# Hybrid decoder step on one core: the decode update in the second half of its stage, the first output weights ahead of their inputs, the key norms' end and the last mixer tail some places later, the weight pool at lower addresses

## Chip, core and metric

The kernel runs on one core of one Trainium2 chip. The metric is the device time of one launch in microseconds (us), lower being better. The time of the kernel before is the median of three runs.

## What is computed

One inference step of two layers over 1,040 prompt tokens (16 learned meta tokens and 1,024 own ones) and 8 decode tokens, width 1,024, everything in float32. Layer 0 mixes tokens by a causal convolution module, layer 1 by RWKV-7 time mixing; each is followed by a squared-ReLU MLP of inner width 4,096. Only layer 1's mixer is touched here. Cut to what matters:

```python
def _wkv7_step(S, inp):                      # one token, per head: S is 64 x 64
    r_t, w_t, k_t, v_t, kk_t, a_t = inp
    sa = jnp.einsum('bhvk,bhk->bhv', S, -kk_t)
    S = (S * w_t[:, :, None, :] + sa[..., None] * (kk_t * a_t)[:, :, None, :]
         + v_t[..., None] * k_t[:, :, None, :])
    return S, jnp.einsum('bhvk,bhk->bhv', S, r_t)
# in _rwkv7: r, k, v, decay, a, g are projections of the shifted input
    kk = kk / jnp.maximum(jnp.sqrt(jnp.sum(kk * kk, axis=-1, keepdims=True)), L2_EPS)   # key norms
    S_final, ys = lax.scan(_wkv7_step, S0, xs)
    yn = ((y - mu) * lax.rsqrt(var + GN_EPS)).reshape(B, T, D_MODEL) * gn_g + gn_b
    out = ((yn + bonus) * g) @ w_o
# in _trunk
    h = h + out
    h = h + _sqrelu_mlp(_rmsnorm(h, norm_mlp[i]), w_mlp_in[i], w_mlp_out[i])
```

The prompt starts from a zero state; each of the 8 decode sequences brings its own state of 16 heads of 64 x 64, and takes one step of the recurrence. That one step is called the decode update below.

## The kernel before

**Matrix products.** A large product is made of three matmuls per 128 x 128 block: high half by high half, high by low, low by high (lines 187, 188, 189). A weight block of 512 KB is loaded on SP's queue into a `raw` tile (line 146), its high half is cast by ACT (`hi`, one operation, line 157), and its low half is subtracted by POOL in four operations of 256 columns (`lo`, line 162). There are five tiles of each kind, so that the load of a block on SP waits until POOL has split the block five places earlier, and all that stands behind that load on SP waits too. TensorE's instructions are called PE, VectorE's DVE, ScalarE's ACT, GpSimd's POOL, SyncE's SP.

**Order.** In layer 1 TensorE's instructions stand in the order in which the program writes them (`in_order`). The other engines' instructions are put in order by a scheduler that works on estimated times when the kernel is built. Every engine runs its queue strictly in that order, DMA issues included.

**Layer 1, first part (about 1,128 to 1,828 us).** `mixer_in(g)` makes the projections r, k, v and the small ones for the four token groups of `G1` (272, 256, 256, 264 columns). Between the projections' matmuls, at fill points, run pieces of earlier work: `tick` advances the recurrence of the prompt, which is worked out in 17 chunks (chunk 0 the meta tokens, then 64 tokens each), `invert` the small inverses that it needs, `norm_gates` the normalisation, bonus and gate of finished tokens. `keys(g)` makes the key norms of a group: squares on ACT, their sums `pn` on TensorE, then a square root, a reciprocal and the two halves `r16h`, `r16l` that `spread` later takes for `pb`. It runs one group ahead of its use. `carry["tail"]()` ends the last pair of heads of a group: it transposes v (`vt_7`), makes the 32 x 32 products of the key vectors (`nn_7`) and the bonus sums (`pk_7`), and writes them out to memory (`d_v`, `d_n`, `d_bv`).

In a chunk of the recurrence A (two banks for each four pairs of heads) are the products of the chunk's vectors; DVE masks them into `xa` and `nr` (lines 1200, 1202); `gg`, `bT`, `po`, `W`, `U`, `S` and `Y` follow on TensorE with copies on ACT and DVE and `sw` on POOL between them.

**Layer 1, second part (about 1,842 us to the end).** `mixer_out(g, ...)` loads the gated output z of a group of `G2` (328, 352, 352 columns) from memory, splits it, multiplies it by `rwkv_w_o` (`ps_oo_0` to `ps_oo_7`, eight weight blocks) and adds it to h. Then comes the MLP: 32 blocks j, for each an inner product `ps_in`, the activation `r`, `s` (line 342 on DVE, ACT), its halves `hh`, `hl` (line 141) and eight outer products `out` that DVE adds to h (line 355). Two blocks j are called a pair here: 96 matmuls of TensorE, four weight blocks, ten operations of lines 342 and 355 and two of line 141 on DVE. The first stage takes group 0 alone (`mixer_out(0)` and an MLP for it); the second makes `mixer_out(1)`, `mixer_out(2)` and one MLP for both.

At the time of the first stage the recurrence's last chunks, the decode update and most norm gates are still to be done. `filler` deals them out over 208 fill points in three streams side by side: the recurrence `until(NCH - 1)`, `decode_step()` with a budget of 82, and `norm_gates` of the groups 1 and 2. `decode_step` transposes the decode vectors (four `pdd`), then updates the state in 16 slices: nine DVE operations of 128 x 256 each (lines 1383 to 1391: seven of two tensors, `TENSOR_TENSOR`, and two reductions), one load before and one store behind on SP. Its output is needed only by the last norm gate.

Of the kernel before, what the change touches and what calls it, by code (L numbers as in the profile page):

```python
# [16 lines left out]
P = 128  # L17
D = 1024
KT = D // P
# [16 lines left out]
N2 = 352  # L36
# [12 lines left out]
def hybrid_step(tc, x_prompt, x_sample, state_conv, state_shift, state_wkv, meta_tokens,  # L49
# [8 lines left out]
    nc = tc.nc  # L58
    ctx = ExitStack()
    with ctx:  # L60
        def pool(stack, name, bufs, **kw):
            return stack.enter_context(tc.tile_pool(name=name, bufs=bufs, reuse_waits="tile", **kw))
# [46 lines left out]
        for name, ap in vecs:  # L109
            n = ap.shape[0]  # L110
# [10 lines left out]

        cur = {}

        def open_tmp(stack, nmax, tag, bufs=3, **kw):
            cur["n"] = cur["wide"] = nmax
            cur["tmp"] = pool(stack, f"tmp{tag}", bufs, **kw)
            cur["stat"] = pool(stack, f"stat{tag}", 1, **kw)

        def stat(name, tag, bufs, w=None):
            return cur["stat"].tile([P, w or cur["n"]], F32, name=name, tag=tag, bufs=bufs)  # L130
# [622 lines left out]
        def spread(ps, r, p):  # L753

            for i, part in enumerate(r):
                nc.tensor.matmul(ps, hspread[:, p].rearrange("p q i -> p (q i)"), part, start=i == 0, stop=i == 1)
# [105 lines left out]
        def proj(w, act, n, name, fill=None):  # L862
            ps = bank(f"p{name}")
            for k in range(KT):
                nc.tensor.matmul(ps[:, :n], w[:, k, :], act[k], start=k == 0, stop=k == KT - 1)  # L865
                if fill and k in (2, 5):
                    fill()
            return ps

        def keys(g, fill):  # L870

            c0, n = G1[g]
            nm = lambda s, *a: f"{s}{g}" + "".join(f"_{x}" for x in a)
            mix = prep[g][0]
            act = [mix(2, k) for k in range(KT)]
            pn = bank(nm("pn"), "x")
            add_pn = lambda: None

            def to_pn(p, sq):
                return lambda: nc.tensor.matmul(pn[:, :n], head_sel(p), sq[:, :n], start=p == 0, stop=p == KT - 1)  # L880
            for p in range(KT):
                yield
                ps = proj(next(wrkv), act, n, nm("k", p), fill)
                k_ = pr.tile([P, N1], F32, name=nm("st", p), tag="st", bufs=2)
                nc.scalar.copy(k_[:, :n], ps[:, :n])
                nc.scalar.dma_start(d_k[:, p, c0:c0 + n], k_[:, :n])
                sq = pr.tile([P, N1], F32, name=nm("sq", p), tag="rk", bufs=2)
                nc.scalar.activation(sq[:, :n], ps[:, :n], AF.Square, scale=vec("k_k", p))
                add_pn()
                add_pn = to_pn(p, sq)  # L890
            r16 = lorap.tile([P, N1], F32, name=nm("r16"), tag="lf")
            r16p = norm[g] = [lorap.tile([P, N1], F32R, name=nm("r16" + q), tag="r16" + q, bufs=2)[:, :n] for q in "hl"]
            add_pn()
            nc.vector.tensor_scalar(r16[:, :n], pn[:, :n], L2_EPS * L2_EPS, None, op0=ALU.max)
            nc.scalar.activation(r16[:, :n], r16[:, :n], AF.Sqrt)
            nc.vector.reciprocal(r16[:, :n], r16[:, :n])
            split(*r16p, r16[:, :n], nc.vector)
        carry = {"tail": lambda: None}

        def mixer_in(g, tick):  # L900
# [80 lines left out]
            gate(wg)  # L981
            carry["tail"]()
            act_v = mixed(3)
            r16p = norm.pop(g)
            ks = iter(())

            def finish(p, rk, ab, vv):
                def trace():
# [56 lines left out]
            late, later = (lambda: lambda: None), lambda: None  # L1045
            for p, rk2 in ahead_of(fetch):
                both()
                ps = proj(next(wrkv), act, n, nm("r", p), both)
                nc.scalar.copy(rk2[:, 2, :n], ps[:, :n])
                if p == 0:  # L1050
                    decay_rate(ww)
# [17 lines left out]
                later = late()  # L1069
                nkk, kp, rp = (rk2[:, i, :] for i in range(3))  # L1070
                pb = bank(nm("pb", p))
                spread(pb[:, :n], r16p, p)
                nc.vector.scalar_tensor_tensor(nkk[:, :n], kp[:, :n], nvec("k_k", p), pb[:, :n], op0=ALU.mult, op1=ALU.mult)
                nc.vector.tensor_tensor_scan(cum[:, :n], smask[:, :n], cum[:, :n], 0.0, op0=ALU.mult, op1=ALU.add)
                em = t_("em", p, "em", 2)
# [37 lines left out]
                if g < 3:  # L1113
                    if p == 0:
                        for _ in ranked(PP, prepare(g + 1)):
                            pass
                        ks = keys(g + 1, both)
                        next(ks)
                    for _ in keys_of(p):
                        next(ks, None)  # L1120
# [49 lines left out]
        def front(c):  # L1170

            xa = xas[c % 2]
            for q in range(2):
                nc.sync.dma_start(xa[HALF[q], :, q, :], d_ab[c, HALF[q], :, 0, :])
            bk = w_([P, KT, P], "bk", c)
            nc.sync.dma_start(bk[HALF[0]], d_ab[c, HALF[0], :, 1, :])
            for i in range(2):
                nc.sync.dma_start(bk[HALF[1], :, i * HS:(i + 1) * HS], d_ab[c, HALF[1], :, 1, (1 - i) * HS:(2 - i) * HS])
            nr, no = w_([P, KT, 2, HS], "nr", c, bufs=2), w_([P, KT, 32], "no", c)
            p32 = w_([P, KT, 32], "p32", c, bufs=2)  # L1180
            nc.sync.dma_start(p32, d_p[c].rearrange("k r t -> r k t"))

            vt = w_([P, KT, HS], "vt", c)
            for q in range(2):
                nc.sync.dma_start(vt[HALF[1 - q]], d_v[c * HS:(c + 1) * HS, :].rearrange("t (k q v) -> q t k v", q=2, v=HS)[q])
            yield RW[0]
            mask = lambda x: m_ar[:, x].unsqueeze(1).broadcast_to([P, 4, HS])
            for j in range(0, KT, 4):
                ps = [bank(f"A{c}{j}{q}", "w") for q in range(2)]
                for i in range(4):  # L1190
                    for q in range(2):
                        nc.tensor.matmul(ps[q][:, i * P:(i + 1) * P], bk[HALF[q], j + i, :], xa[HALF[q], j + i, q, :],
                                         start=True, stop=True, tile_position=(64 * q, 0))
                pv = [t.rearrange("p (i x) -> p i x", x=P) for t in ps]
                js = slice(j, j + 4)
                for q in range(2):
                    nc.scalar.copy(no[Q[2 * q], js, :], pv[q][Q[2 * q], :, 32:64])
                for q in range(2):
                    r_k = HALF[1 - q]
                    nc.vector.tensor_mul(xa[r_k, js, q, :HS], pv[q][r_k, :, :HS], mask(slice(0, HS))[r_k])  # L1200
                for q in range(2):
                    nc.vector.tensor_mul(nr[:, js, q, :], pv[q][:, :, HS:], mask(slice(HS, P)))
                if j == 0:
                    yield RW[1]
            x32 = w_([P, KT, 32], "x32", c)
            nc.vector.transpose(flat(x32), flat(p32))
            chunks[c] = xa, bk, nr, no, p32, x32, vt
            yield RW[2]

# [262 lines left out]
        with in_order():  # L1472
            shift_in()
            for _ in prepare(0):
                pass
            for _ in keys(0, lambda: None):
                pass
            for g in range(4):
                mixer_in(g, lambda slow=1.0: tick(g, slow))
            carry["tail"]()  # L1480
            while invert():
                pass
            advance(CHUNK_WAIT * NCH, NEED[GN_OF[0][-1]])
            for _ in ng0:
                pass
# [1 line left out]


        with ExitStack() as l1:
            open_tmp(l1, N2, "2", 3)  # L1490
            actp = pool(l1, "actp1", 1)
            open_weights(l1, 0, {"w": 5}, "f")
            residp = pool(l1, "resid1", 1)
            hidp = pool(l1, "hidp1", 2)
            open_ep(l1, "f", ey=2)
# [4 lines left out]
            def mixer_out(g, residp, actp, fill, add):  # L1500
                lo, n = G2[g]
                h1 = hl[g] = residp.tile([P, KT, cur["wide"]], F32, name=f"h1_{g}", tag="h")
                nc.sync.dma_start(h1[:, :, :n], d_h[:, :, lo:lo + n])
                z = new_acts(actp, f"z{g}", cur["wide"])
                for p in range(KT):
                    t = tt(f"zr{g}{p}", "t1")
                    nc.sync.dma_start(t[:, :n], d_z[:, p, lo:lo + n])
                    split(z[0][p][:, :n], z[1][p][:, :n], t[:, :n], nc.vector)
                for m in range(KT):
                    ps = dense(load_col(rwkv_w_o[0], m, f"wo{g}_{m}", nc.gpsimd), z, n, f"oo{g}_{m}", fill)  # L1510
                    nc.vector.tensor_add(h1[:, m, :n], h1[:, m, :n], ps[:, :n])
                    add(m, h1[:, m, :n])
                    fill()
# [57 lines left out]
            def group(g, actp, hidp, sums):  # L1571
# [2 lines left out]
                return (g, hv, n, *mlp_in(actp, hv, n, 1, f"m1{g}", sums), hidp)  # L1574


            ng2 = norm_gates(GN_OF[2])
            fill, rest = filler(2 * KT + MLP_POINTS,
                                ([until(NCH - 1)], FA * CHUNK_WAIT * (NCH - 1 - st["done"])),
                                ([decode_step()], 82), ([norm_gates(GN_OF[1]), ng2], NGA))  # L1580
            add, sums = sums_of(0)
            with in_order():
                mixer_out(0, residp, actp, fill, add)
# [61 lines left out]
```

## Time and profile before

| | before |
|---|---|
| median of three runs | 2812.3 us (2811.88 to 2817.02) |
| the profiled execution | 2817.97 us |
| its span, first to last instruction | 2816.3 us |
| TensorE busy in the span | 2661.4 us |
| DVE busy | 1776.7 us |
| POOL busy | 1499.7 us |
| ACT busy | 1180.9 us |
| mean granted TensorE clock | 0.972 |

A busy time is the union of an engine's instructions. An operation's length on DVE or POOL includes time in which it has started and is held up, so the same operation can have several lengths. Waits are put down to what came last before the engine went on.

### The profile page before, as it was taken

How to read it: one execution, taken by the hardware profiler on the slowest of the kernel's cores; microseconds unless marked ns; L12 is line 12 of the kernel's file. 1: busy time of each engine (PE TensorE's matmuls, PEld its weight loads, DVE VectorE, ACT ScalarE, POOL GpSimd, SP SyncE). 2: the span in 40 equal slices, each digit the busy share in tenths (PEclk: the TensorE clock that was granted, in tenths of full speed). 3: DMA queues.
4: the chain of work that ended last, by engine and by line, in shares of the span. 5: the costliest groups of instructions: out<-in, count | busy, mean ns of one | idle time of the engine just before them, and what ended most of it. 6: DMA issues, size and time to landing. Idle time of an engine off the chain costs nothing.

```text
span 2816.3 us, 51957 instructions
## 1 busy us (share of the span) xinstructions
PE 2661.4 (95%) x19866; PEld 2510.5 (89%) x19866; DVE 1776.7 (63%) x3518; ACT 1180.9 (42%) x2167; POOL 1499.7 (53%) x2066
## 2 busy tenths in 40 slices
PE   8999999999999899998999999978899999999998
PEld 7998999999999899787787777768789999999998
DVE  5999999996455545233756555488985554444444
ACT  5545444544355333233444453545444452222223
POOL 6676877887788775021111112365568773333332
PEclk9999999999999999999999999979999999999999
DMA  6663544454445642667767766766675642222211
GB/s 178 175 183 90 157 136 135 128 181 135 142 134 157 183 140 83 199 201 203 192 178 199 205 161 181 205 187 177 166 211 154 180 119 86 68 70 73 69 53 42
DMA packets 615863, 416.45 MB, mean 148 GB/s; under 512 B 104936, under 2 KB 558760, under 8 KB 615614
## 3 DMA queue, kind: packets, MB, share of 16 engines
q1 hardware_dynamic: 565996, 367.36, 46.2%
q10 hardware_dynamic: 41090, 19.93, 2.7%
q0 software_dynamic: 8528, 25.83, 2.6%
q8 instruction: 157, 2.57, 0.4%
q14 instruction: 92, 0.75, 0.1%
HBM read 345.60 MB, written 68.37 MB: 147 GB/s over the span
## 4 chain that ended last, share of the span: by engine, by line
PE 72%; DVE 13%; DMA 6%; issue 3%; ACT 3%; POOL 2%; SPq 0%; ACTq 0%; DVEq 0%; POOLq 0%
PE out L187 8%; PE ps_in L189 8%; PE ps_in L187 8%; PE out L189 8%; PE ps_in L188 8%; PE out L188 8%; PE pk L865 3%; PE pr L865 3%; PE pv L865 2%; DVE cv L519 1%; POOL wo_lo L162 1%; PE ps_o L189 1%; DVE tt L1153 1%; PE ps_o L188 1%; PE ps_o L187 1%
## 5 line engine op out<-in xcount | busy, mean ns | idle before, releaser
L162 POOL TENSOR_TENSOR wo_lo<-wo_raw,wo_hi 128x256 fp32r<-128x256 f32 x736 | 564.9, 799 | 259.3 <-ACT wo_hi L157 258.6
L162 POOL TENSOR_TENSOR wi_lo<-wi_raw,wi_hi 128x256 fp32r<-128x256 f32 x640 | 490.1, 798 | 285.5 <-ACT wi_hi L157 267.8
L187 PE MATMUL out<-hh,wo_hi 128*128 128x352 f32 (+2 forms) x1536 | 503.2, 328 | 20.7 <-DVE h L355 9.3
L355 DVE TENSOR_TENSOR h<-h,out 128x352 f32<-128x352 f32 (+2 forms) x768 | 387.3, 510 | 196.8 <-PE out L189 196.4
L189 PE MATMUL out<-hl,wo_hi 128*128 128x352 f32 (+2 forms) x1536 | 494.2, 324 | 7.2 <-DVE hl L141 7.2
L187 PE MATMUL ps_in<-m_h,wi_hi 128*128 128x352 f32 (+2 forms) x1536 | 496.2, 323 | 2.6 <-DVE h L355 2.6
L188 PE MATMUL out<-hh,wo_lo 128*128 128x352 f32 (+2 forms) x1536 | 496.0, 323 | 0.0
L189 PE MATMUL ps_in<-m_l,wi_hi 128*128 128x352 f32 (+2 forms) x1536 | 494.6, 322 | 0.1
L188 PE MATMUL ps_in<-m_h,wi_lo 128*128 128x352 f32 (+2 forms) x1536 | 492.7, 321 | 0.0
L519 DVE SCALAR_TENSOR_TENSOR cv<-u,wdw,cv 128x352 f32<-128x352 f32 (+2 forms) x720 | 376.5, 571 | 0.7
L157 ACT CAST wi_hi<-wi_raw 128x1024 fp32r<-128x1024 f32 x160 | 167.9, 1050 | 398.2 <-PE out L189 198.7
L157 ACT CAST wo_hi<-wo_raw 128x1024 fp32r<-128x1024 f32 x184 | 192.6, 1049 | 316.2 <-PE out L189 154.9
L187 PEld LDWEIGHTS out<-hh,wo_hi 128*128 128x128 f32 x1536 | 293.3, 191 | 26.9 <-DVE h L355 11.7
L189 PEld LDWEIGHTS out<-hl,wo_hi 128*128 128x128 f32 x1536 | 291.2, 190 | 8.9 <-DVE hl L141 8.8
L187 PEld LDWEIGHTS ps_in<-m_h,wi_hi 128*128 128x128 f32 x1536 | 290.0, 189 | 5.2 <-issue 1.7
L188 PEld LDWEIGHTS out<-hh,wo_lo 128*128 128x128 f32 x1536 | 292.8, 191 | 0.6
L188 PEld LDWEIGHTS ps_in<-m_h,wi_lo 128*128 128x128 f32 x1536 | 289.4, 188 | 0.9
L189 PEld LDWEIGHTS ps_in<-m_l,wi_hi 128*128 128x128 f32 x1536 | 288.6, 188 | 1.2 <-DVE m_l L285 0.4
L342 DVE SCALAR_TENSOR_TENSOR r<-ps_in,rs_m 128x352 f32<-128x352 f32 (+2 forms) x192 | 98.2, 515 | 243.3 <-PE ps_in L189 238.1
L141 DVE TENSOR_TENSOR hl<-s,hh 128x352 fp32r<-128x352 f32 (+2 forms) x192 | 147.9, 772 | 104.5 <-ACT hh L140 104.3
L344 ACT ACTIVATE s<-r 128x352 f32<-128x352 f32 (+2 forms) x192 | 93.6, 490 | 128.9 <-DVE r L342 128.5
L1030 POOL DMA_DIRECT2D d_n<-n x32 | 24.4, 764 | 212.9 <-DVE n L1020 141.0
(355 smaller groups left out, 4909.3 us busy)
## 6 DMA issues: line engine op xcount, KB each, us to landing
wi_raw<-in_w_mlp_in_dram SPq DMA_DIRECT2D x160, 512.0 KB
wo_raw<-in_w_mlp_out_dram SPq DMA_DIRECT2D x160, 512.0 KB
wk_raw<-in_rwkv_w_k_dram SPq DMA_DIRECT2D x32, 512.0 KB
wr_raw<-in_rwkv_w_r_dram SPq DMA_DIRECT2D x32, 512.0 KB
wv_raw<-in_rwkv_w_v_dram SPq DMA_DIRECT2D x32, 512.0 KB
d_ab<-ab POOLq DMA_DIRECT2D x32, 512.0 KB, 4.8
pg_raw<-in_conv_w_pw_dram SPq DMA_DIRECT2D x24, 512.0 KB
pa_raw<-in_conv_w_pw_dram SPq DMA_DIRECT2D x24, 512.0 KB
```

Of the source, the lines that this page charges most:

```text
L141: eng_lo.tensor_sub(lo, src, hi.bitcast(F32))
L157: nc.scalar.copy(hi[:, :a * b], raw[:, :a * b])
L162: eng_lo.tensor_sub(lo[:, cs], raw[:, cs], hi[:, cs].bitcast(F32))
L187: nc.tensor.matmul(ps, w[0], act[0], start=first, stop=False)
L188: nc.tensor.matmul(ps, w[1], act[0], start=False, stop=False)
L189: nc.tensor.matmul(ps, w[0], act[1], start=False, stop=last)
L342: nc.vector.scalar_tensor_tensor(r[:, :n], ps[:, :n], 0.0, rs()[:, :n], op0=ALU.max, op1=ALU.mult)
L344: nc.scalar.activation(s[:, :n], r[:, :n], AF.Square)
L355: nc.vector.tensor_add(hv[:, 4 * i + m, :], hv[:, 4 * i + m, :], ps[:, :n])
L519: nc.vector.scalar_tensor_tensor(acc[m][:, :n], ug[:, m, j:j + n], wdw[:, m, j:j + 1], acc[m][:, :n], op0=ALU.mult, op1=ALU.add)
L865: nc.tensor.matmul(ps[:, :n], w[:, k, :], act[k], start=k == 0, stop=k == KT - 1)
L1153: nc.vector.tensor_mul(o, ni[:, :j, j:j + 1].broadcast_to([B, j, wd]), ni[:, j:j + 1, j + 1:top].broadcast_to([B, j, wd]))
```

## The change

Five things are moved; what is computed stays the same.

1. **Decode update.** `late_start(DL)` puts 120 empty units ahead of `decode_step()`, and the stream's budget is DL + DN = 230 instead of 82, so the decode update is dealt out over the last part of the first stage.
2. **Key norms' end.** A `yield` cuts `keys` ahead of the last sum, square root, reciprocal and halves; that end runs in `first()`, at the first fill point within the r projection of the next `mixer_in`.
3. **Transposed x.** `x32` is made ahead of the masks of a chunk rather than behind them.
4. **Last mixer tail.** Four ticks of the recurrence run before the last `carry["tail"]()`.
5. **First output weights.** The weight blocks of `mixer_out` are asked for two ahead, the first two before z is loaded; the weight pool is opened directly behind the scratch pool, at lower addresses, and the pool of statistics behind it.

```diff
+        def open_tmp(stack, nmax, tag, bufs=3, stats=True, **kw):
...
+            if stats:
+                cur["stat"] = pool(stack, f"stat{tag}", 1, **kw)
...
                 add_pn = to_pn(p, sq)
+            yield
             r16 = lorap.tile([P, N1], F32, name=nm("r16"), tag="lf")
...
-            r16p = norm.pop(g)
-            ks = iter(())
+            ks, kend = iter(()), carry["keys"]
+
+            def first():
+                both()
+                next(kend, None)
...
-                ps = proj(next(wrkv), act, n, nm("r", p), both)
+                ps = proj(next(wrkv), act, n, nm("r", p), both if p else first)
...
-                spread(pb[:, :n], r16p, p)
+                spread(pb[:, :n], norm[g], p)
...
-                        ks = keys(g + 1, both)
+                        ks = carry["keys"] = keys(g + 1, both)
...
             yield RW[0]
+            x32 = w_([P, KT, 32], "x32", c)
+            nc.vector.transpose(flat(x32), flat(p32))
...
-            x32 = w_([P, KT, 32], "x32", c)
-            nc.vector.transpose(flat(x32), flat(p32))
             chunks[c] = xa, bk, nr, no, p32, x32, vt
...
-            for _ in keys(0, lambda: None):
-                pass
+            carry["keys"] = keys(0, lambda: None)
+            for _ in range(KT + 1):
+                next(carry["keys"])
             for g in range(4):
                 mixer_in(g, lambda slow=1.0: tick(g, slow))
+            for _ in range(4):
+                tick(3, 1.0)
             carry["tail"]()
...
-            open_tmp(l1, N2, "2", 3)
+            open_tmp(l1, N2, "2", 3, False)
+            open_weights(l1, 0, {"w": 5}, "f")
             actp = pool(l1, "actp1", 1)
-            open_weights(l1, 0, {"w": 5}, "f")
+            cur["stat"] = pool(l1, "stat2", 1)
...
+                block = lambda m: load_col(rwkv_w_o[0], m, f"wo{g}_{m}", nc.gpsimd)
+                ws = [block(m) for m in range(2)]
                 z = new_acts(actp, f"z{g}", cur["wide"])
...
-                    ps = dense(load_col(rwkv_w_o[0], m, f"wo{g}_{m}", nc.gpsimd), z, n, f"oo{g}_{m}", fill)
+                    if m + 2 < KT:
+                        ws.append(block(m + 2))
+                    ps = dense(ws.pop(0), z, n, f"oo{g}_{m}", fill)
...
+            DL, DN = 120, 110
+
+            def late_start(n):
+                for _ in range(n):
+                    yield 1
...
-                                ([decode_step()], 82), ([norm_gates(GN_OF[1]), ng2], NGA))
+                                ([late_start(DL), decode_step()], DL + DN), ([norm_gates(GN_OF[1]), ng2], NGA))
```

Line numbers of the kernel after are up to eleven higher: line 141 becomes 142, 342 becomes 343, 355 becomes 356, and the decode update's 1383 to 1391 become 1388 to 1396.

DVE around block 20 of the first stage's MLP, before: `r_20`, `r_21` are the activations of blocks 20 and 21, `hl` their low halves, `out_9` the outer products of the two blocks before.

```order
2825 L342 SCALAR_TENSOR_TENSOR r_20_0_23266<-ps_in_20_0_23241,rs_m_20453 128x328
2826 L141 TENSOR_TENSOR hl_20_23240<-s_20_0_23268,hh_20_23239 128x328
2827 L342 SCALAR_TENSOR_TENSOR r_21_0_23306<-ps_in_21_0_23281,rs_m_20453 128x328
2828 L355 TENSOR_TENSOR h_0_19706<-h_0_19706,out_9_0_0_23321 128x328
2829 L355 TENSOR_TENSOR h_0_19706<-h_0_19706,out_9_0_1_23329 128x328
2830 L141 TENSOR_TENSOR hl_20_23240<-s_21_0_23308,hh_20_23239 128x328
2831 L355 TENSOR_TENSOR h_0_19706<-h_0_19706,out_9_0_2_23337 128x328
```

The same place of DVE's queue in the kernel after; `t`, `sa`, `Sdec` belong to the decode update.

```order
2694 L343 SCALAR_TENSOR_TENSOR r_20_0_23175<-ps_in_20_0_23137,rs_m_20543 128x328
2695 L1388 TENSOR_TENSOR t_23247<-Sdec_23246,dq 128x256
2696 L1389 TENSOR_REDUCE sa<-t_23247 128x4
2697 L1390 TENSOR_TENSOR Sdec_23246<-Sdec_23246,dq 128x256
2698 L1391 TENSOR_TENSOR t_23247<-sa,dq 128x256
2699 L142 TENSOR_TENSOR hl_20_23136<-s_20_0_23177,hh_20_23135 128x328
2700 L1392 TENSOR_TENSOR Sdec_23246<-Sdec_23246,t_23247 128x256
2701 L1393 TENSOR_TENSOR t_23247<-dq 128x256
2702 L343 SCALAR_TENSOR_TENSOR r_21_0_23215<-ps_in_21_0_23190,rs_m_20543 128x328
2703 L1394 TENSOR_TENSOR Sdec_23246<-Sdec_23246,t_23247 128x256
2704 L356 TENSOR_TENSOR h_0_19797<-h_0_19797,out_9_0_0_23230 128x328
```

Before, the 144 decode operations stand between `r_2` and `r_14`, among those of the recurrence and the norm gates. After, they stand between `r_18` and the end of the last pair, with no recurrence and few norm gates among them: 20 to 22 for each pair.

SP's queue at the start of the first stage, before: `zr` are the eight inputs of `mixer_out(0)`, `wo_4` its fifth weight block, `ni` the inputs of the last inverses.

```order
579 L1507 DMA zr_19724<-d_z 128x328
580 L1507 DMA zr_19728<-d_z 128x328
581 L1507 DMA zr_19732<-d_z 128x328
582 L146 DMA wo_4_raw<-in_rwkv_w_o_dram 128x8x128
583 L1507 DMA zr_19736<-d_z 128x328
584 L1507 DMA zr_19740<-d_z 128x328
585 L1507 DMA zr_19744<-d_z 128x328
586 L1507 DMA zr_19748<-d_z 128x328
587 L1507 DMA zr_19752<-d_z 128x328
588 L1147 DMA ni_19568<-d_n 128x1024
```

The same place after; `wo_5` to `wo_7` are the last blocks of `mixer_out(0)`, `wi` the first of the MLP, `ey` the inputs of norm gates.

```order
580 L1518 DMA zr_19841<-d_z 128x328
581 L147 DMA wo_4_raw<-in_rwkv_w_o_dram 128x8x128
582 L147 DMA wo_5_raw<-in_rwkv_w_o_dram 128x8x128
583 L147 DMA wo_6_raw<-in_rwkv_w_o_dram 128x8x128
584 L147 DMA wo_7_raw<-in_rwkv_w_o_dram 128x8x128
585 L147 DMA wi_0_0_raw<-in_w_mlp_in_dram 128x8x128
586 L147 DMA wi_0_1_raw<-in_w_mlp_in_dram 128x8x128
587 L1152 DMA ni_19659<-d_n 128x1024
588 L1512 DMA h_0_19797<-d_h 128x8x328
589 L1437 DMA ey_0_19961<-d_y 128x512
590 L1437 DMA ey_1_20218<-d_y 128x512
591 L1518 DMA zr_19845<-d_z 128x328
```

Five weight loads, `ni`, h and two `ey` now stand between the third and the fourth input z, where one weight load stood; each of the five waits for POOL's split of the block five places earlier.

TensorE at the same boundary, after: what stands between the last `pb_7` of the projections and the first output product.

```order
8042 L757 MATMUL pb_7_19511<-r16l_18173,hspread 128x264
8043 L1265 MATMUL W_19535<-sv,xa_12568 64x64 x16
8044 L1235 MATMUL po_19557<-p_19199,gg_19427 32x32 x16
8045 L1281 MATMUL U_19589<-w_19552,p_19430 64x64 x16
8046 L1199 MATMUL A_19610<-xa_12567,bk_19578 128x128
...
8053 L1199 MATMUL A_19611<-xa_12567,bk_19578 128x128
8054 L1006 MATMUL vt_7_19628<-ident,vv_7_19477 128x128 x2
8055 L1023 MATMUL nn_7_19635<-ab_7_19527 32x32 x16
8056 L1039 MATMUL pk_7_19654<-rk_7_19525,hsum 128x264
8057 L188 MATMUL ps_oo_0_19874<-z_h_19817,wo_0_hi 128x328
```

Before, `pb_7` is followed by `vt_7`, `nn_7`, `pk_7` and `ps_oo_0` directly, and `W`, `po`, `U`, the eight A and what belongs to them come behind the fourth input of `ps_oo_0`.

More of the change, by code (lines that the diff above doesn't have):

```diff
@@ L122, in hybrid_step @@
         cur = {}
-        def open_tmp(stack, nmax, tag, bufs=3, **kw):
+        def open_tmp(stack, nmax, tag, bufs=3, stats=True, **kw):
             cur["n"] = cur["wide"] = nmax
             cur["tmp"] = pool(stack, f"tmp{tag}", bufs, **kw)
-            cur["stat"] = pool(stack, f"stat{tag}", 1, **kw)
+            if stats:
+                cur["stat"] = pool(stack, f"stat{tag}", 1, **kw)
         def stat(name, tag, bufs, w=None):
```

## The prediction

> **What bounds the kernel now.** First the page: the shares of the engines and the slices.
>
> ```profile
> span 2816.3 us, 51957 instructions
> PE 2661.4 (95%) x19866; PEld 2510.5 (89%) x19866; DVE 1776.7 (63%) x3518; ACT 1180.9 (42%) x2167; POOL 1499.7 (53%) x2066
> PE   8999999999999899998999999978899999999998
> DVE  5999999996455545233756555488985554444444
> ```
>
> TensorE sets the time, with 155 us of its span idle. The idle time is thickest in slices 27 to 29, where DVE is fullest: the start of the first stage. So next the windows, cut at the stages (engine busy times, granted clock, DMA):
>
> ```profile
> core 0: us, PE busy (x) PEld busy (x) DVE busy (x) ACT busy (x) POOL busy (x), PEclk, DMA share, GB/s
> 1360.00:1820.00 460.00, 430.89 (x4886) 357.93 (x4886) 263.30 (x598) 213.56 (x524) 87.18 (x162) 0.97 0.71 187
> 1820.00:1905.00 85.00, 63.39 (x661) 57.58 (x662) 65.53 (x124) 41.53 (x81) 50.73 (x67) 0.82 0.72 193
> 1905.00:2110.00 205.00, 182.45 (x2043) 170.70 (x2041) 182.97 (x362) 97.91 (x184) 119.38 (x136) 0.95 0.68 185
> 2110.00:2210.00 100.00, 98.30 (x651) 97.59 (x651) 51.17 (x95) 42.21 (x63) 84.37 (x112) 1.00 0.53 158
> ```
>
> The third row holds the decode update: PE idles 22.6 of 205 us at a clock of 0.95, and DVE is 89% busy. The fourth row is the second half of the stage: PE nearly full, DVE half empty, POOL 84% busy. PE's waits in the third stretch say who is late:
>
> ```profile
> PE bT L1253 <- DVE nr L1202: 9.0, 5, 3.6
> PE Y L1292 <- DVE nr L1202: 4.0, 2, 2.8
> ```
>
> 13.0 of the 22.6 us end with DVE's mask `nr`: the recurrence is behind work queued on DVE.
>
> **Decode, first half.** What leaves that stretch, from the groups of DVE in 1860 to 2110 (the first and the last of seven two-tensor lines, and both reductions):
>
> ```profile
> L1390 DVE TENSOR_TENSOR t<-Sdec,dq 128x256 f32<-128x256 f32 x16 | 10.7, 672 | 0.2
> L1389 DVE TENSOR_TENSOR Sdec<-Sdec,t 128x256 f32<-128x256 f32 x16 | 8.1, 505 | 0.1
> L1384 DVE TENSOR_REDUCE sa<-t 128x4 f32<-128x256 f32 x16 | 6.6, 412 | 0.3
> L1391 DVE TENSOR_REDUCE yd<-t 128x4 f32<-128x256 f32 x16 | 6.5, 408 | 0.2
> ```
>
> Seven lines between 8.1 and 10.7 us and two of 6.5 make 78 us in 144 operations. DVE's load falls from 183 to 105 us in 205. From 1360 to 1820, where DVE is 57% busy and the recurrence runs too, PE idles 29 us in 460, most of it for the projections' own inputs (below); so I leave 5 us of the 22.6 in place. The lower clock costs 0.05 x 182 = 9 us; fewer gaps should return 7. Gain 17.5 + 7 = 24.5 us, between 13 (the `nr` waits alone) and 31.
>
> **Decode, second half.** Here the decode update meets POOL's splits. How the same operation fares beside a split and without one, from DVE's and POOL's timeline (start, length):
>
> ```profile
> 2046.07 3.21 POOL L162 TENSOR_TENSOR wi_lo<-wi_raw,wi_hi 128x256 fp32r<-128x256 f32 x4 [2.27 <-issue]
> 2046.11 0.97 DVE L1387 TENSOR_TENSOR Sdec<-Sdec,t 128x256 f32<-128x256 f32 x1
> 2049.24 4.15 POOL L162 TENSOR_TENSOR wo_lo<-wo_raw,wo_hi 128x256 fp32r<-128x256 f32 x4
> 2053.03 0.40 DVE L1391 TENSOR_REDUCE yd<-t 128x4 f32<-128x256 f32 x1
> 2053.95 0.41 DVE L1383 TENSOR_TENSOR t<-Sdec,dq 128x256 f32<-128x256 f32 x1
> ```
>
> A two-tensor operation costs 0.41 us alone and up to about 1 us beside a split; the reduction costs 0.40 us even inside one. A batch of four splits takes 3.2 to 4.2 us here; undisturbed it takes 2.8 (row at 210.21 below). The Trainium skill ("SBUF — State Buffer", "Who interferes with whom") says that a DVE instruction with two SBUF inputs contends with a GpSimd instruction that reads SBUF, and that a reduction does not; by that rule the second half, where splits are densest, is the worse place for these operations, and these rows agree with it.
>
> The order puts 21.5 decode operations into each pair of blocks. The nearest thing in the trace is the pair from `r_12` to `r_14`, which held 21; behind it a pair without any:
>
> ```profile
> 2066.76 0.49 DVE L342 SCALAR_TENSOR_TENSOR r<-ps_in,rs_m 128x328 f32<-128x328 f32 x1
> 2087.73 0.49 DVE L342 SCALAR_TENSOR_TENSOR r<-ps_in,rs_m 128x328 f32<-128x328 f32 x1
> ...
> 2134.32 0.50 DVE L342 SCALAR_TENSOR_TENSOR r<-ps_in,rs_m 128x328 f32<-128x328 f32 x1 [3.10 <-PE ps_in L189]
> ...
> 2148.72 0.50 DVE L342 SCALAR_TENSOR_TENSOR r<-ps_in,rs_m 128x328 f32<-128x328 f32 x1 [3.10 <-PE ps_in L189]
> ```
>
> 20.97 us against 14.40. DVE ran without a gap through the first, but it also held two operations of the recurrence and four of norm gates of 512 columns, which leave; one of them, from the groups of DVE:
>
> ```profile
> L1439 DVE TENSOR_REDUCE ems<-ey 128x8 f32<-128x512 f32 x7 | 4.8, 679 | 1.3 <-DMA ey<-d_y 1.3
> ```
>
> Six at 0.68 are 4.1 us; 16.9 us remain. So DVE becomes the bound: 2.5 us more for each of 144 / 21.5 = 6.7 pairs, +17 us. Ends: without a split beside them 21.5 operations of 0.41 take 8.8 us, and the MLP's own twelve, at 0.50 as in the row at 2134.32, 6.0: 14.8 us a pair, a loss of 3; at the full 20.97 us the loss is 44. I take 17 because that pair lies nearest.
>
> The 16 loads and 16 stores of the states move along SP's queue with it, among weight loads that run five blocks (18 us of PE) ahead; the store waits for DVE, and the weights behind it have that cover. At the stage's end the last norm gates wait for the last decode slice, and the inputs of `mixer_out(1)` for those: +3 us (0 to 8; the chunk of norm gates costs 16 operations there, eleven before).
>
> **The boundary at 1830 to 1882.** Edits 4 and 5 meet here. What TensorE, SP, ACT and POOL do there now (waits; then starts and lengths):
>
> ```profile
> PE ps_oo L187 <- ACT wo_hi L157: 4.8, 1, 4.8
> PE nn L1018 <- DVE ab L1105: 3.4, 1, 3.4
> PE vt L1001 <- ACT vt L1003: 3.0, 1, 3.0
> ```
>
> ```profile
> 1832.01 5.85 SPq L1507 DMA_DIRECT2D zr<-d_z  x5
> 1841.40 0.32 SPq L1147 DMA_DIRECT2D ni<-d_n  x1
> 1841.50 4.83 ACT L157 CAST wo_hi<-wo_raw 128x1024 fp32r<-128x1024 f32 x5
> 1842.62 14.97 POOL L162 TENSOR_TENSOR wo_lo<-wo_raw,wo_hi 128x256 fp32r<-128x256 f32 x20 [2.88 <-ACT wo_hi L157]
> ```
>
> These 11.2 us of waits go: the casts of `wo` now stand ahead of those of z, and W, po, U and eight A fill the time of the v, n and k waits. But z inputs 4 to 8 stand behind five weight loads, each held by a split of an earlier block. With the splits starting at about 1833 instead of 1842.6, the fifth ends near 1847; `ni`, h, two `ey` (issue and transfer) follow, and input 4 arrives near 1857 and is split on DVE near 1860, behind inverses. TensorE, through with three inputs at about 1842, then waits some 18 us. The recurrence work that stood at 1851 to 1880 is by then done or follows with its inputs ready, so that I find both kernels at the same place, the fourth output block, near 1882: 0 us. The ends are -8 (five splits done earlier let `ni` pass earlier) and +14 (the 18 us less the 4.8 of `ps_oo`).
>
> **Key norms, x32.** What stands for their waits in the first part, in TensorE's waits:
>
> ```profile
> PE l_w L964 <- ACT lw L954: 6.7, 1, 6.7
> PE pn L880 <- ACT sq L888: 5.6, 4, 3.4
> ```
>
> The last `pn` moves 20 to 31 places later and its square is then long done: -5.6, of which some returns because the square root's table load and `r16` move into the r projection, ahead of the scan and `pb`. Together -3 (between -8 and +3). The transposed x ahead of the masks puts 0.4 us before `nr`, inside slack once DVE has room: 0.
>
> **Sum.** -24.5 + 17 + 3 + 0 - 3 = -7.5 us on the profiled execution's own 2817.97 us, which stands 5.7 above the median. I move the median by the same amount: 2812.3 - 7.5 = 2804.8 us. 0.2%, or 5.6 us, is what a measurement of this kernel can tell from no change.
>
> **The rivals.** *Slower, by a shared port in the second half.* If POOL's batches starve two-tensor operations, a pair takes the whole 20.97 us: -24.5 + 44 + 3 - 3 = +19.5, 2832 us. It decides from 18.3 us a pair on (equal to before), and it is slower by over 0.2% from 19.1. For it speaks one row of the convolution, where a two-tensor addition lasted through POOL's splits, of which the last batch is shown:
>
> ```profile
> 202.56 10.85 DVE L230 TENSOR_TENSOR acc_mu<-acc_mu,u 128x352 f32<-128x352 f32 x1
> 210.21 2.81 POOL L162 TENSOR_TENSOR pg_lo<-pg_raw,pg_hi 128x256 fp32r<-128x256 f32 x4
> ```
>
> Against it: in 2046 to 2050 no operation waited longer than one split. The same page of the skill calls the port an exclusive lock, held for the whole instruction, with the loser fully blocked. As a mechanism of this kernel, without starving: 16 splits of 0.70 and 19 two-tensor operations (17 of the decode update, two `hl`) of 0.35 make 17.9 us a pair, a loss of 23 us and a net -1, 2811 us: no change.
>
> *Slower, by late inputs.* The boundary's +14 with the rest of the sum: +6.5, 2819 us. It decides if `S`, `Y` and A of the last ticks, which stand behind the fourth input, are again what the first blocks wait for.
>
> *Faster, decode hidden.* If the splits hardly hold the operations up, a pair takes the 14.8 us above (loss 3, not 17): -21.5, 2791 us. For it: DVE is half idle there, and reductions do not suffer. Against it: the 20.97 us pair.
>
> **How the numbers follow.** Forecast 0.41, starving port 0.16, plain lock 0.14, late inputs 0.12, decode hidden 0.17. The forecast's own range is 2797 to 2810; 0.33 of its 0.41 lie below 2806.7. Faster: 0.33 + 0.17 + 0.02 of the lock = 0.52. Same: 0.08 + 0.11 + 0.02 = 0.21. Slower: 0.16 + 0.10 + 0.01 = 0.27. The range leaves out the outer part of the starving port and of the hidden decode: 2785 to 2827.
>
> **What would show it.** Right: in 1905 to 2100 waits for `nr` nearly gone and DVE near 55%; then pairs of 16 to 18 us with DVE full, POOL's batches at 3.2 us and more. Wrong: pairs of 14.4 us (decode hidden) or of 19 and more (port); first output blocks that end after 1905; a new wait of over 8 us at `mixer_out(1)`.

## The result

| | before | after |
|---|---|---|
| median of ten runs | 2815.77 us (2811.88 to 2818.16) | 2808.04 us (2803.01 to 2814.99) |
| ratio to before | 1 | 0.9973, 95% interval 0.9962 to 0.9983 |
| span of the profiled execution | 2816.3 us | 2802.6 us |

The kernel after is faster by 0.27%, or 7.7 us of the medians; the forecast was 7.5. The time forecast, 2804.8 us, lies 3.2 us under the measured median, within its range: the three runs it started from have a median of 2812.3 us, 3.5 under that of all ten. The two profiled executions lie 13.7 us apart. 3.7 to 4.2 of these arise in layer 0, where TensorE's order is the same in both, so I count them as chance.

The page of the kernel after:

```profile
span 2802.6 us, 51913 instructions
PE 2647.2 (94%) x19866; PEld 2497.0 (89%) x19866; DVE 1777.7 (63%) x3518; ACT 1183.1 (42%) x2169; POOL 1496.2 (53%) x2066
PE   8999999999999899998998999969999799999998
DVE  5999999996455545233756555576769754434444
```

A slice is 70 us long here. DVE's fullest slices were 27 to 30; now it is 31, and 27 to 30 are at 6 and 7. PE's dent of slices 27 to 29 is now slice 27 alone, the boundary, and a new one stands in slice 32, at the end of the stage. The windows of before, cut the same way in the kernel after:

```profile
1820.00:1905.00 85.00, 58.84 (x669) 53.89 (x670) 70.04 (x132) 35.54 (x68) 47.49 (x64) 0.82 0.62 170
1905.00:2110.00 205.00, 197.80 (x2083) 187.75 (x2082) 138.78 (x258) 108.26 (x199) 135.14 (x168) 1.00 0.70 190
2110.00:2210.00 100.00, 85.49 (x522) 81.08 (x521) 95.19 (x193) 34.49 (x49) 75.22 (x88) 0.94 0.57 167
```

The stretch that held the decode update has 7.2 us of idle PE instead of 22.6, at a clock of 1.00 instead of 0.95; the next has 14.5 instead of 1.7. TensorE's waits, first in 1905 to 2110, then in 2090 to 2240:

```profile
PE out L188 <- DVE r L343: 3.1, 2, 2.1
PE bT L1258 <- DVE nr L1209: 2.1, 2, 1.5
```

```profile
PE out L188 <- DVE r L343: 9.1, 7, 2.1
PE yn L1422 <- DVE ey L1451: 8.1, 1, 8.1
```

`nr` ended 13.0 us of waits and ends 2.1. In its place DVE's activation `r` is late once a pair, and the stage's last transposes wait 8.1 us for the norm gate behind the last decode slice.

Lengths of stages, from the starts of `pb` on TensorE and of `r` on DVE in each profile (us); `late_only` is the kernel before with the first edit alone, `early` the kernel after without it:

| | before | after | late_only | early |
|---|---|---|---|---|
| first to last `pb`, the projections | 639.1 | 632.7 | 639.7 | 632.7 |
| last `pb` to `r_0`, the boundary | 86.2 | 98.1 | 85.9 | 101.2 |
| `r_0` to `r_18` | 206.7 | 168.3 | 175.9 | 194.1 |
| `r_18` to `r_31` | 95.7 | 117.5 | 119.7 | 95.2 |
| `r_31` to the end | 599.2 | 601.5 | 602.8 | 599.5 |

Of the boundary's 11.9 us about 8 are work that moved: at `r_0` the kernel after has done one more round of U, S, Y and 16 A.

### The profile page after: what moved, and what is told of

Its sections match the earlier page's. It is cut to its first block, busy times and chain, and to the rows that moved or that the text cites. A ratio compares the mean times of both kernels' runs of the same rounds, so it can differ in the third digit from the quotient of the medians.

```text
span 2802.6 us, 51913 instructions
## 1 busy us (share of the span) xinstructions
PE 2647.2 (94%) x19866; PEld 2497.0 (89%) x19866; DVE 1777.7 (63%) x3518; ACT 1183.1 (42%) x2169; POOL 1496.2 (53%) x2066
## 4 chain that ended last, share of the span: by engine, by line
PE 72%; DVE 15%; DMA 6%; ACT 3%; issue 2%; POOL 1%; SPq 0%; ACTq 0%; DVEq 0%; POOLq 0%
PE ps_in L188 8%; PE out L188 8%; PE ps_in L190 8%; PE ps_in L189 8%; PE out L189 8%; PE out L190 8%; PE pk L866 4%; PE pr L866 3%; PE pv L866 2%; DVE cv L520 2%; DVE h L356 1%; PE ps_o L190 1%; DVE tt L1158 1%; PE ps_o L189 1%; PE ps_o L188 1%
## 5 line engine op out<-in xcount | busy, mean ns | idle before, releaser
L1035 POOL DMA_DIRECT2D d_n<-n x32 | 24.5, 765 | 204.6 <-DVE n L1025 130.9
```

## The experiments

Ratios are to the kernel before, with 95% intervals.

**The late start alone, and everything but it.** `late_only` is the kernel before with this, `early` the kernel after with the opposite:

```diff
-                                ([decode_step()], 82), ([norm_gates(GN_OF[1]), ng2], NGA))
+                                ([late_start(DL), decode_step()], DL + DN), ([norm_gates(GN_OF[1]), ng2], NGA))
```

> The kernel before with the decode update's late start alone. Theory: mixers and boundary as before, the first half 26 to 34 us shorter, the pairs from r_18 on at 17 to 18 us: 4 to 8 us faster than before. Rival, that late decode needs the ticks done earlier to pay: first half shorter by less than 20 us, no gain in all, or slower by up to 5 us.

> The kernel after with the decode update's late start taken out again (budget 82), the other four edits kept. Theory: late decode frees about 26 us between the first output block and r_18, and gives back 21.7 us in the pairs from r_18 to r_31; so with the decode early again the first half (r_0 to r_16) goes from 154 us back to about 180 and the pairs behind r_18 from 17.4 back to 14.4 us: 4 to 8 us slower than the kernel after, so within 3 us of the kernel before. Rival, that the gain is the mixers' (11 us earlier at the end of the projections) and late decode is worth nothing in the end: the same time as the kernel after, about 8 us faster than before.

Measured: `late_only` 2815.92 us, 0.9998 (0.9988 to 1.0007); `early` 2809.06 us, 0.9971 (0.9961 to 0.9981). The rivals' times, not the theory's: the late start alone gains nothing that can be measured, and without it the kernel keeps its gain. The reason that the rival of `late_only` gave is not what happened: both halves of the mechanism are there, with no ticks done earlier. That of `early`, a gain in the projections, is what the next experiment finds. `r_0` to `r_18` and `r_18` to `r_31`, first of before, then of `late_only`:

```profile
1914.70:2121.40 206.70, 182.55 (x2022) 171.31 (x2023) 184.06 (x369) 99.17 (x187) 124.49 (x140) 0.95 0.68 185
2121.40:2217.10 95.70, 95.70 (x640) 95.70 (x640) 44.13 (x83) 38.43 (x53) 79.49 (x108) 1.00 0.50 149
```

```profile
1914.60:2090.50 175.90, 172.35 (x2018) 163.59 (x2019) 114.59 (x221) 97.62 (x187) 112.30 (x139) 1.00 0.72 189
2090.50:2210.20 119.70, 104.40 (x655) 99.39 (x653) 111.62 (x224) 41.27 (x54) 93.69 (x113) 0.99 0.55 161
```

30.8 us are gained, 24.0 given back at once, 3.6 behind the stage. The 3.2 us that are left in this one profile are too few for the runs to tell from nothing.

**The key norms' end alone** (before with the second edit):

```diff
+            yield
             r16 = lorap.tile([P, N1], F32, name=nm("r16"), tag="lf")
...
-                ps = proj(next(wrkv), act, n, nm("r", p), both)
+                ps = proj(next(wrkv), act, n, nm("r", p), both if p else first)
```

> The kernel before with the second edit alone: the key norms' last sum, square root, reciprocal and halves at the first fill point of the next group's r projection. Theory, that this edit carries most of the gain: the four waits for pn (5.6 us) go and nothing comes back for them, the projections take 633 us from the first to the last pb instead of 639, and the kernel is 5 to 8 us faster than before, about as fast as the kernel after. Rival, that the square root's table load and r16 only come late elsewhere: 0 to 3 us faster.

Measured: 2808.32 us, 0.9964 (0.9951 to 0.9978). This edit alone gains as much as the whole change does. The third group's projections, of before and then of `keys_only`:

```profile
1527.30:1730.70 203.40, 185.46 (x2023) 154.36 (x2022) 113.65 (x254) 94.57 (x224) 31.48 (x51) 0.95 0.69 180
```

```profile
1526.10:1725.60 199.50, 184.18 (x2023) 153.41 (x2022) 115.45 (x258) 94.73 (x225) 31.21 (x51) 0.96 0.69 184
```

Every group is shorter, by 1.6, 2.1, 3.9 and 1.1 us. The row `pn <- ACT sq` (5.6 us) is gone from TensorE's waits, and no new row of that size has come, though `pb <- ACT vv` went from 11.1 to 13.5 us. The four stages behind the projections agree with those of before within 0.9 us each, so the gain arises here. By the ratio it is 10 us, more than the theory's 5 to 8. In the profiles of the twelve kernels here that have this edit, whatever else they have, the projections take 624.6 to 633.3 us, mean 628.5; in the two without it 639.1 and 639.7. The transposed x was not run alone.

**No weights ahead, and no ticks.** The kernel after without its fifth edit, and without its fourth:

```diff
-                ws = [block(m) for m in range(2)]
...
-                    ps = dense(ws.pop(0), z, n, f"oo{g}_{m}", fill)
+                    ps = dense(block(m), z, n, f"oo{g}_{m}", fill)
```

```diff
-            for _ in range(4):
-                tick(3, 1.0)
             carry["tail"]()
```

> The kernel after without its fifth edit: output weights asked for one at a time, z loaded first, pools in the old place. Theory, that the weights ahead only trade the wait for weights (4.8 us before) for a wait for z (5.7 and 10.6 us after): the z waits go, a wait for wo_hi of about 5 us comes back, r_0 moves by -6 to +2 us, all in all 0 to 6 us faster than the kernel after. Rival, that the lower pool and the weights ahead give the mixers' last group its 5 us: the last group is 5 us later and the whole 3 to 8 us slower than the kernel after.

> The kernel after without its fourth edit: no four ticks ahead of the last mixer tail. Theory, that the ticks fill waits of vt_7 and nn_7 that otherwise stand idle (3.0 and 3.4 us before): these waits come back, 3 to 8 us slower than the kernel after, and r_0 is no earlier although one chunk's U, S, Y and A (about 8 us of TensorE) are left for later. Rival, that the tail was hidden behind late z anyway: within 2 us of the kernel after.

Measured: `no_ahead` 2806.9 us, 0.9963 (0.9950 to 0.9976); `no_ticks` 2804.23 us, 0.9955 (0.9941 to 0.9969). Neither edit gains; the ticks may cost some 4 us (the intervals overlap), which no expectation had. TensorE's waits between the last `pb` and 1905, in the kernel after, then without ticks, then without weights ahead (to 1900):

```profile
PE ps_oo L188 <- ACT z_h L141: 10.6, 1, 10.6
PE U L1281 <- ACT p L1274: 6.0, 2, 4.4
PE ps_oo L190 <- DVE z_l L142: 5.7, 1, 5.7
```

```profile
PE ps_oo L188 <- ACT z_h L141: 17.8, 3, 11.6
PE nn L1023 <- DVE ab L1110: 5.0, 1, 5.0
```

```profile
PE A L1199 <- DVE fs L1308: 14.6, 2, 7.4
PE U L1281 <- DVE w L1267: 5.1, 1, 5.1
PE ps_oo L188 <- ACT wo_hi L158: 1.9, 1, 1.9
```

The wait for the fourth z is there with and without ticks, as SP's order has it; the ticks trade `nn` for `U`. Without the weights ahead the waits for z go, as the theory of `no_ahead` had it, but what comes back is less a wait for `wo_hi` (1.9 us, not 5) than one of the recurrence's A for DVE's `fs`.

**Decode update in PSUM.** The kernel after with the decode vectors and the scratch tile in PSUM, where POOL's splits do not read; the order of DVE stays as it is within a few places:

```diff
-                dq = dk.tile([P, 6, HS], F32, name="dq")
-                nc.scalar.dma_start(dq, d_dec.rearrange("i b (h c) -> (b h) i c", c=HS))
+                dqs = dk.tile([P, 6, HS], F32, name="dqs")
+                nc.scalar.dma_start(dqs, d_dec.rearrange("i b (h c) -> (b h) i c", c=HS))
+                dq = bank("dq", "x")[:, :6 * HS].rearrange("p (i c) -> p i c", c=HS)
+                nc.scalar.copy(dq, dqs)
...
-                    t4 = rows(dk.tile([P, HV * HS], F32, name=f"t4{hv}", tag="t4"))
+                    t4 = rows(bank(f"t4{hv}", "w")[:, :HV * HS])
...
-                    nc.vector.tensor_mul(t4, overk(dq[:, 5, vs]), overv(1))
+                    nc.vector.tensor_mul(t4, overk(dqs[:, 5, vs]), overv(1))
```

> The kernel after, with the decode update's vectors dq and its scratch tile t4 in PSUM instead of SBUF, so that each of its two-tensor operations has at most one tensor in SBUF; nothing else is moved. Theory, that the loss behind r_18 is DVE waiting beside POOL's splits: each operation takes about 0.41 us inside a batch as outside, POOL's batches fall from 3.4 to under 3.1 us, r_18 to r_31 goes from 117.5 to 97 to 102 us, and the kernel is 14 to 20 us faster than the kernel after. Rival, that 21.5 operations a pair are too many at any length, or that the states' loads and stores hold SP up: r_18 to r_31 stays above 110 us and the time within 5 us of the kernel after.

Measured: 2792.02 us, 0.9909 (0.9895 to 0.9922), and `r_18` to `r_31` in 102.5 us, both within the theory. That stretch, in the kernel after and then with PSUM:

```profile
2083.60:2201.10 117.50, 104.31 (x655) 99.48 (x654) 111.76 (x225) 41.19 (x54) 93.24 (x112) 0.99 0.55 161
```

```profile
2086.70:2189.20 102.50, 100.11 (x654) 98.11 (x653) 87.59 (x227) 40.48 (x54) 78.13 (x109) 1.00 0.62 184
```

One and the same addition `Sdec + t` (the dearest line of the kernel after), and POOL's splits, in the groups of the kernel after:

```profile
L1394 DVE TENSOR_TENSOR Sdec<-Sdec,t 128x256 f32<-128x256 f32 x16 | 12.0, 751 | 0.3
L163 POOL TENSOR_TENSOR wo_lo<-wo_raw,wo_hi 128x256 fp32r<-128x256 f32 x68 | 57.6, 876 | 16.2 <-ACT wo_hi L158 15.1 <-DMA dq<-d_dec 1.0
```

and with PSUM:

```profile
L1396 DVE TENSOR_TENSOR Sdec<-Sdec,t 128x256 f32<-128x256 f32 x16 | 6.6, 412 | 0.2
L163 POOL TENSOR_TENSOR wo_lo<-wo_raw,wo_hi 128x256 fp32r<-128x256 f32 x73 | 54.0, 771 | 14.4 <-ACT wo_hi L158 14.4
```

All seven two-tensor lines now take 408 to 424 ns, where they took 548 to 751; the splits of `wo` go from 876 to 771 ns on average. That PSUM is not simply the faster place is seen within the kernel after: of its 112 two-tensor operations there, the 13 that met no split took 412 ns on average. With PSUM the 90 that began beside a split took 418, the longest 430. The number of operations is the same, so their length beside the splits is what most of the second half's loss went to: 15.0 us of 21.8 (117.5 to 102.5, before 95.7). Of the other 6.8 us the cause is not shown; DVE still waits for the states there:

```profile
DVE t L1390 <- DMA Sdec<-in_state_wkv_dram: 5.4, 5, 1.9
```

**Half of the decode slices worked out.**

```diff
+                    if hv % 2 == 0:
-                    nc.vector.tensor_mul(t4, S, overv(2))
+                        nc.vector.tensor_mul(t4, S, overv(2))
...
```

> The kernel after with only every second of the 16 slices of the decode update worked out (the other slices are loaded and stored unchanged, and their outputs left at zero), so half of its 144 DVE operations with all of its DMAs. Theory, that DVE's load is the bound there: about 11 operations a pair at 0.65 us and the MLP's 6 us are 13 us, under the 14.4 of TensorE, so r_18 to r_31 falls from 117.5 to 96 to 100 us. Rival, that the loads and stores on SP among the weights, or POOL, set the pace: it stays above 105 us.

Measured, in a single run of 2800.95 us: `r_18` to `r_31` in 119.2 us, not 96 to 100. The edit did not do what I meant: the scheduler put the 72 operations at the old density between `r_18` and `r_26`, and left none behind. There DVE was busy for no more than 84% of `r_22` to `r_26` (its window first) and waited for states' loads with `r` queued behind them (DVE's waits from `r_18` on):

```profile
2124.90:2160.30 35.40, 27.97 (x171) 26.99 (x171) 29.75 (x62) 11.04 (x15) 23.16 (x30) 0.95 0.56 172
```

```profile
DVE t L1390 <- DMA Sdec<-in_state_wkv_dram: 6.2, 5, 2.5
```

So it tells nothing of fewer operations a pair; it does show that the two pairs from `r_22` to `r_26` can take 17.7 us on average with DVE not full.

**PSUM in other company.** Without ticks; then also with decode early, with 60 and 140 for DL and DN, and without the weights ahead; last, before with only the key norms' end and PSUM.

> Decode update in PSUM as above, and the four ticks ahead of the last mixer tail left out, the other edits kept. Theory, that the ticks cost 3.5 us net and the shared port 17: 17 to 24 us faster than the kernel after, 25 to 32 faster than before. Rival, that the ticks matter only by chance of the run: the same as the kernel with the ticks and PSUM.

> Decode update in PSUM, no four ticks, and the late start taken out (budget 82): in the order its operations now stand from r_6 to r_24, still partly among the recurrence. Theory, that the late start was worth so little only because of the shared port: without the port, decode among the recurrence still delays nr, and the late order keeps an advantage, so this is 4 to 12 us slower than the same kernel with the late start (2790 us). Rival, that without the port the place does not matter: within 3 us of it.

> Decode update in PSUM, no four ticks, late start of 60 units and a budget of 200 instead of 120 and 230: decode from r_12 to r_26, behind the recurrence and ahead of the last pairs. Theory: behind the recurrence any place is as good, and the last norm gates no longer wait for it: 0 to 5 us faster than with 120 and 230 (2790 us). Rival, that the norm gates between r_12 and r_16 are delayed: up to 4 us slower.

> Decode update in PSUM, late start of 120 units, no four ticks and no weights ahead nor lower pool: of the change only the key norms' end, the transposed x and the late start are left. Theory, that the weights ahead trade one wait for another: within 4 us of the kernel with them (2790 us). Rival, that z loaded first saves the 10 us wait for the fourth input: 5 to 10 us faster.

> The kernel before with two things alone: the key norms' end moved (second edit) and the decode update in PSUM, decode in its old place among the recurrence. Theory, that the late start, the transposed x, the weights ahead and the ticks add nothing once the port is free: 0.986 to 0.990 of before, as fast as the fastest so far (0.9878, which has the late start and the transposed x too). Rival, that the late start is worth 5 us or more without the weights ahead: 0.991 of before or slower.

| | median, us | ratio | decode stands |
|---|---|---|---|
| psum_no_ticks | 2790.23 | 0.9901 (0.9888 to 0.9915) | `r_18` to `r_31` |
| psum_early | 2791.74 | 0.9909 (0.9893 to 0.9924) | `r_6` to `r_24` |
| psum_mid | 2793.84 | 0.9917 (0.9901 to 0.9932) | `r_11` to `r_26` |
| psum_no_ahead | 2783.32 | 0.9878 (0.9863 to 0.9892) | `r_18` to `r_31` |
| keys_psum | 2792.79 | 0.9903 (0.9887 to 0.9920) | `r_6` to `r_24` |

By ratio, PSUM without ticks gains 20 us on the kernel after, as expected of it. PSUM gains 15 to 18 us wherever there is a run whose edits differ in nothing else: 0.9973 to 0.9909 in the kernel after, 0.9955 to 0.9901 without ticks, 0.9964 to 0.9903 with the key norms' end alone. With PSUM the place of the decode update matters little from `r_6` on: 0.9901, 0.9909 and 0.9917 lie within one interval (that of `psum_early`), against my theories of both a gain and a loss. The place that it had before, `r_2` to `r_14`, is in none of these runs; the scheduler put it further back in `psum_early` and in `keys_psum`, whose expectation has it in its old place. The fastest, 34 us under before, leaves out the weights ahead and the ticks; it is the rival's 5 to 10 us that came, about 6, but its interval just touches that of `psum_no_ticks`, so the size is open. `keys_psum` lies at the edge between its two theories: whether the late start is worth some us without the weights ahead stays open too.

## Why the prediction came out right, point by point

The sum came out right, but that it lies within 0.2 us of the measured gain is luck. The key norms gave some 7 us more than their term, and the late start and the boundary together gave about as much less than theirs.

- **First half, -24.5 us.** Measured on `r_0` to `r_18`: -30.8 (`late_only` to before) and -25.8 (after to `early`). The mechanism (`nr` late behind decode work, and the lower clock) is shown by the waits and the clock of 1.00.
- **Second half, +17 us.** Measured +24.0 and +22.3. The step that failed is the pair of 16.9 us: the pairs took 16.0 to 19.5, mean 17.4 up to `r_30`, and the last, from `r_30` to `r_31`, 13.1 instead of 10.8. Here are the first and the last `r` of one pair and how two of its operations fared beside a batch of splits:

```profile
2103.09 0.49 DVE L343 SCALAR_TENSOR_TENSOR r<-ps_in,rs_m 128x328 f32<-128x328 f32 x1
2105.62 3.40 POOL L163 TENSOR_TENSOR wo_lo<-wo_raw,wo_hi 128x256 fp32r<-128x256 f32 x4 [1.61 <-ACT wo_hi L158]
2105.74 0.95 DVE L1392 TENSOR_TENSOR Sdec<-Sdec,t 128x256 f32<-128x256 f32 x1
2106.72 0.83 DVE L1393 TENSOR_TENSOR t<-dq 128x256 f32<-128x256 f32 x1
2119.49 0.48 DVE L343 SCALAR_TENSOR_TENSOR r<-ps_in,rs_m 128x328 f32<-128x328 f32 x1
```

  16.4 us. No operation here waits through a whole batch, so the starving rival fell; the plain lock's 17.9 us a pair lies as near as my 16.9. That the cause is two operands in SBUF beside POOL's splits is shown by PSUM. Two figures of the starving rival were added up wrongly: by its own terms it is level with before at 14.4 + 24.5 / 6.7 = 18.1 us a pair, not 18.3, and slower by 0.2% from 18.9, not 19.1. The measured 17.4 lies under both. The rule of the Trainium skill ("SBUF — State Buffer", "Who interferes with whom"), that two SBUF inputs contend with a GpSimd read and one does not, agrees: 751 against 412 ns.
- **Behind the stage, +3 us.** Measured +3.6 and +2.0; the wait of 8.1 us for `ey` was foreseen in kind. It is also, just, the wait of over 8 us that was named as a sign of being wrong; the stage's end lost no more than its term allowed.
- **The boundary, 0 us (-8 to +14).** The wait for the fourth z came, 10.6 us and not 18. One of 5.7 us for `z_l` ahead of it was not foreseen, so 16.3 us of waits for z stand where 11.2 us went. By the stages from the last `pb` to `r_18`, which count the moved work on both sides, the other edits cost 4.6 us (266.4 in the kernel after, 261.8 in `late_only`) or 2.4 (295.3 in `early`, 292.9 before). By the runs neither ticks nor weights ahead gain (0.9973 with both, 0.9955 and 0.9963 without one).
- **Key norms, -3 us (-8 to +3).** The mis-sized term: -6.4 in the two profiles, -8.7 in `keys_only`, -10 by its ratio (0.9964), past the end of its range. I let some of the 5.6 us come back. In `keys_only` 2.4 may have, in the waits of `pb`, but the gap had cost clock too, as the turn to the fourth group shows, before and after:

```profile
1685.00:1730.70 45.70, 42.31 (x339) 35.84 (x338) 16.43 (x39) 13.12 (x26) 5.83 (x9) 0.96 0.68 170
```

```profile
1680.00:1720.20 40.20, 40.20 (x338) 34.56 (x337) 17.25 (x42) 13.07 (x27) 5.70 (x9) 1.00 0.77 193
```

  5.5 us for a wait of 3.4.
- **The net of the late start, -4.5 us,** which carried the forecast, is what the runs do not bear out: `late_only` puts it between -3.4 and +2.0, and by the ratios `early` lies 0.6 us from the kernel after. By the profiles' stages, boundary included, it is -3.5 (`late_only`) and -4.6 (`early`, 3.1 of it in the boundary). Which of the two is nearer stays open within the runs' spread.

## What to carry to other kernels

Moving work from a crowded stretch to an idle one pays only what its operations still cost there: price them beside the engine that is busy in the new place, from rows of that company. If a DVE operation is slowed by POOL, putting one of its two inputs into PSUM can take more off (here 18 us, 0.9973 to 0.9909) than moving it. And a short wait of TensorE that recurs with every group is worth more than its own length when the clock falls with it, as at the turn to the fourth group here: 5.5 us for 3.4, at 0.96 instead of 1.00.

## What was not expected of the hardware

- The same DVE addition of 128 x 256 takes 412 ns with one input in PSUM and 751 ns on average with both in SBUF, where POOL is busy for 79% of the time. POOL's subtractions gain too: those of `wo` took 771 ns with PSUM and 876 without.
- Projections with the same order of TensorE's instructions took between 624.6 and 633.3 us from one kernel's profile to the next, so single profiles do not resolve edits of a few us there.
